# A hybrid decoder step on one core: attention products in three rounded passes, index keys by chunk, sample products at every second tile

## The chip, the cores and the metric

The kernel runs on one core of one Trainium2 chip. Its time is what the device takes for one execution, in microseconds (us). PE is the matrix engine (PEld its loads of the stationary operand), DVE the vector engine, ACT the scalar engine, POOL the general one (GpSimd), SP the engine that issues transfers; SPq, PEq and the like are the sequencers of these engines.

## The reference

One layer of a decoder trunk is applied to a prompt of 2048 tokens and to 8 single-token samples with paged caches. All is float32. What matters here, cut from the reference:

```python
qkv, z, beta_in, a_in, aq, ak, av, iq, ik, iw = split(h @ w_in, cuts)      # h: normed, modulated x
o_gdn = gated delta rule(conv(qkv), ...)                                   # 4 heads of 128
# sparse attention, 4 query heads on 2 key heads of 128, by blocks of 128 queries
score = einsum('bqh,bqhs->bqs', iw, relu(einsum('bqhd,bsd->bqhs', iq, ik)))   # 8 index heads of 64
_, idx = top_k(where(key_pos <= qpos, score, -inf), 256)
p = softmax(q @ k[idx] * 128 ** -0.5);  o_att = p @ v[idx]
x = x + ga1 * (concat(o_gdn, o_att) @ w_out)
x = x + ga2 * ((silu(gate) * up) @ w_ffn_out),  gate, up = split(norm(x) @ w_ffn_in)
```

The kernel does not gather keys: it computes all scores up to the diagonal and adds a bias of -1e30 where a key was not selected.

## The kernel before

**Tiling.** The prompt is worked in four groups of 512 tokens; attention in 16 query blocks of 128. A float32 operand that goes to the large products is split in two parts: `hi`, the value rounded to the format fp32r, and `lo`, the rest. A product is then three passes, hi·hi, hi·lo and lo·hi, in `mm3` (L180, L181, L182). Each weight tile of 128 x 512 is loaded raw (`wr`, two buffers), rounded by ACT (L163) and subtracted by DVE (L164) into `wi` (three buffers). One weight tile feeds four banks of PSUM: 12 matmuls of 512 columns, called a tile below.

**Stages.** Phase 1, up to about 1400 us of the span, projects the four groups, runs the delta rule and attends query blocks 0 to 3 (`first_attn`, which borrows buffers of the delta rule). Phase 2 is three streams that are woven together: the output and feed-forward tiles of groups 0 to 2 (`ffn`, the feed), the index scores and top-k of blocks 4 to 15 (`index`), and their attention (`attend`). The samples' own steps run beside them. Group 3's feed comes last, alone, from about 3130 us, since it needs the attention of block 15. With it the samples' rows go through the same weights.

**Attention (`attend`).** For each of two key heads and each chunk of up to 512 keys, two query heads are multiplied in plain float32 (L1671); the DVE adds the bias and takes the maximum out of PSUM (L1672); ACT takes the exponential. Then, for every two key blocks, PE transposes the four probability tiles into a PSUM bank (L1700), ACT copies the bank to `PT` (L1703), and PE multiplies the values in plain float32, one matmul of 256 columns per key block (L1688). The values of a pair come one pair later (`held`), so that the copy has the time of the next transposes. The values of four key blocks are loaded at a time into `V` (three buffers), a chunk of keys into `kT` (three buffers). The index keys of the whole prompt lie in eight tiles of SBUF that are loaded once, at the start of phase 2.

**Last group.** Each raw weight tile is kept for the samples in a ring of eight buffers (`raw`: `wr`, and `kT` and `V`, which attention no longer needs). `beside` puts four matmuls with 32 stationary columns (L1811) into a list, and `tick`, called after each tile, runs up to two entries of that list.

**What sets the order.** PE's order is written by `weave`: each stream yields its estimated PE time and what it needs of PSUM and of DVE and ACT, and the planner takes the next stream that is ready. The feed may go first while the attention streams have spent more than a share of `PACE` us. PE runs in exactly this order. The other engines take their instructions in the order that a scheduler gives them; each runs its own in order. All transfers are issued by SP, one after the other.

## Time and profile before

| | us |
|---|---|
| median of 3 runs (3690.44 to 3701.23) | 3693.47 |
| the profiled execution's own time | 3695.31 |
| its span, first to last instruction | 3693.2 |
| PE busy in the span | 3430.8 (93%) |
| DVE, ACT, POOL busy | 2083.7, 1476.0, 595.6 |
| mean granted PE clock | 0.967 of full speed |

The profile lists matmul records: a plain float32 matmul leaves two, an fp32r one leaves one. A record's duration is longer than the distance to the next start, since matmuls are pipelined; what one costs a busy PE is read from the starts. In a timeline row `x4` means four records merged.

### The profile page before, as it was taken

To read this page: it belongs to the slowest core of one execution; us is meant where nothing else is said; L and a number is where in the kernel's file an instruction comes from. 1 tells how busy PE (TensorE), PEld (TensorE's weight loads), DVE (VectorE), ACT (ScalarE), POOL (GpSimd) and SP (SyncE) were. 2 spreads that over 40 slices of the span, in tenths; PEclk is the share of its full clock that TensorE was granted. 3 is DMA by queue.
4 is the path that set the end of the run, shared out by engine and by line. 5 is a ranking of instruction groups with operands and counts; after the bars stand their busy time and mean duration, and the time that the engine had idled before them with its cause. 6 is when DMAs were issued, how large, how long until landed. Compare 5 with 4: busy or idle time off the path is not lost.

```text
span 3693.2 us, 62968 instructions
## 1 busy us (share of the span) xinstructions
PE 3430.8 (93%) x23441; PEld 2646.3 (72%) x23441; DVE 2083.7 (56%) x4377; ACT 1476.0 (40%) x2868; POOL 595.6 (16%) x548
## 2 busy tenths in 40 slices
PE   7999999999998898989988999999899999899997
PEld 5867778777766776777766677787677777677775
DVE  3656646636644665666667545666665653443434
ACT  3333323423334323344456534564544633322222
POOL 0001000101001023212210122222022111211213
PEclk8999999999999898999999999999999999999998
DMA  6754565565575225455544453335423233432221
GB/s 240 247 206 164 184 239 190 177 234 180 183 265 189 72 93 162 125 165 155 156 150 141 132 176 104 108 98 175 141 90 98 82 103 106 168 106 81 81 80 62
DMA packets 412270, 545.52 MB, mean 148 GB/s; under 512 B 47364, under 2 KB 285225, under 8 KB 411946
## 3 DMA queue, kind: packets, MB, share of 16 engines
q1 hardware_dynamic: 411954, 541.41, 45.6%
q8 instruction: 186, 3.05, 0.3%
q14 instruction: 130, 1.06, 0.1%
HBM read 435.49 MB, written 124.75 MB: 152 GB/s over the span
## 4 chain that ended last, share of the span: by engine, by line
PE 74%; DVE 9%; DMA 6%; issue 5%; ACT 4%; SPq 1%; POOL 1%; DVEq 0%; ACTq 0%; POOLq 0%
PE d L180 18%; PE d L182 16%; PE d L181 16%; PE s L1626 3%; PE g L1688 3%; PE s L1671 2%; DVE wi L164 1%; PE g L1700 1%; PE g L1811 1%; DVE tm L1768 1%; DMA wi<-kept 1%; ACT bias L1500 1%; PE g L1058 1%; ACT wi L163 1%; PE g L1112 1%
## 5 line engine op out<-in xcount | busy, mean ns | idle before, releaser
L180 PE MATMUL d<-hh,wi 128*128 128x512 f32 x1792 | 780.6, 436 | 32.5 <-DVE tm L1768 15.2
L181 PE MATMUL d<-hl,wi 128*128 128x512 f32 x1792 | 710.2, 396 | 4.7 <-DVE hl L415 3.3
L182 PE MATMUL d<-hh,wi 128*128 128x512 f32 x1792 | 709.8, 396 | 0.0
L164 DVE TENSOR_TENSOR wi<-wr,wi 128x512 fp32r<-128x512 f32 x537 | 394.5, 735 | 485.4 <-ACT wi L163 478.5
L163 ACT CAST wi<-wr 128x512 fp32r<-128x512 f32 x537 | 332.2, 619 | 788.7 <-PE d L182 558.0
L180 PEld LDWEIGHTS d<-hh,wi 128*128 128x128 f32 x1792 | 342.3, 191 | 133.4 <-issue 27.7
L182 PEld LDWEIGHTS d<-hh,wi 128*128 128x128 f32 x1792 | 341.2, 190 | 77.8 <-DVE wi L164 0.8
L181 PEld LDWEIGHTS d<-hl,wi 128*128 128x128 f32 x1792 | 343.1, 191 | 73.3 <-issue 9.1
L1769 POOL TENSOR_TENSOR xt<-xt,tm 128x512 f32<-128x512 f32 x192 | 279.0, 1476 | 433.5 <-DVE tm L1768 384.4
L180 PE MATMUL d<-wi,hh 128*128 128x512 f32 x768 | 325.3, 424 | 24.6 <-DMA wi<-kept 11.0
L180 PE MATMUL d<-wi,ah 128*128 128x512 f32 x704 | 302.6, 430 | 20.0 <-DVE tm L1768 9.0
L181 PE MATMUL d<-wi,hh 128*128 128x512 f32 x768 | 301.8, 393 | 0.4 <-DVE wi L164 0.4
L182 PE MATMUL d<-wi,hl 128*128 128x512 f32 x768 | 302.2, 393 | 0.0
L182 PE MATMUL d<-wi,al 128*128 128x512 f32 x704 | 282.7, 401 | 3.3 <-POOL al L1940 2.6
L181 PE MATMUL d<-wi,ah 128*128 128x512 f32 x704 | 282.1, 401 | 0.0
L1940 POOL TENSOR_TENSOR al<-ca,ah 128x512 fp32r<-128x512 f32 x88 | 119.3, 1369 | 847.1 <-ACT ah L1939 577.5
L1635 DVE SCALAR_TENSOR_TENSOR sc<-rl,iw,sc 128x512 f32<-128x512 f32 (+3 forms) x224 | 167.5, 748 | 80.4 <-ACT rl L1628 74.6
L1628 ACT ACTIVATE rl<-s 128x512 f32<-128x512 f32 (+3 forms) x288 | 150.1, 544 | 147.0 <-PE s L1626 137.0
L180 PEld LDWEIGHTS d<-wi,hh 128*128 128x128 f32 x768 | 145.4, 189 | 74.2 <-DMA wi<-kept 16.5
L1768 DVE TENSOR_TENSOR tm<-d,row 128x512 f32<-128x512 f32 x224 | 152.1, 685 | 69.0 <-PE d L182 49.4
L180 PEld LDWEIGHTS d<-wi,ah 128*128 128x128 f32 x704 | 135.1, 192 | 69.8 <-DVE tm L1768 15.5
L1500 ACT ACTIVATE bias<-sc,sv 128x640 bf16<-128x640 f32 (+11 forms) x120 | 169.7, 1414 | 27.1 <-DVE sv L1502 12.8
(529 smaller groups left out, 5449.8 us busy)
## 6 DMA issues: line engine op xcount, KB each, us to landing
wi<-kept SPq DMA_DIRECT2D x168, 512.0 KB
wr<-in_w_ffn_in_dram SPq DMA_DIRECT2D x572, 128.0 KB
wr<-in_w_ffn_out_dram SPq DMA_DIRECT2D x143, 256.0 KB
kept<-wi SPq DMA_DIRECT2D x56, 512.0 KB
xt<-in_x_prompt_dram SPq DMA_DIRECT2D x8, 2048.0 KB
row<-in_w_ada_dram SPq DMA_DIRECT2D x32, 512.0 KB
wr<-in_w_in_dram SPq DMA_DIRECT2D x56, 256.0 KB
kT<-kT_d SPq DMA_DIRECT2D x54, 256.0 KB
```

What stands on the lines that cost most here:

```text
L163: nc.scalar.copy(w[:, 0], wr)
L164: nc.vector.tensor_tensor(w[:, 1], wr, w[:, 0].bitcast(F32), op=OP.subtract)
L180: self.o(nc.tensor.matmul(out, wh, xh, start=start, stop=False, **kw))
L181: self.o(nc.tensor.matmul(out, wh, xl, start=False, stop=False, **kw))
L182: self.o(nc.tensor.matmul(out, wl, xh, start=False, stop=stop, **kw))
L1500: nc.scalar.activation(c, s, AF.Sign, bias=t, accum_out=cnt)
L1626: self.o(nc.tensor.matmul(ps[:, :w], iq[:, h, :].bitcast(F32R), B["ikT"][c * 2 + a][:, :w].bitcast(F32R), start=a == 0, stop=a == 1))
L1628: nc.scalar.activation(r[:, :w], ps[:, :w], AF.Relu)
L1635: nc.vector.scalar_tensor_tensor(s, r[:, :w], iw, s, op0=OP.mult, op1=OP.add)
L1768: nc.vector.tensor_tensor(tm, pd, rw, op=OP.mult)
L1769: (nc.vector if soon else nc.gpsimd).tensor_tensor(xt, xt, tm, op=OP.add)
L1940: nc.gpsimd.tensor_tensor(al[b], a, ah[b].bitcast(F32), op=OP.subtract)
```

## The change

**Attention in three passes.** In phase 1 the keys and values are split when they are projected: ACT rounds (two copies of 256 columns per token block), POOL subtracts (two), and both parts go to DRAM (`kT_d` and `V_d` double). `attend` splits a block's queries once (ACT into `qh`, POOL in place) and calls `mm3` for the scores and for the values. The probabilities are rounded by ACT's copy out of PSUM, and a new DVE subtraction (L1704) writes their low part into the second half of `PT`.

**Buffers and transfers.** `kT` now holds both parts of a chunk (two buffers for three), `V` both parts of two key blocks for four (three buffers, a transfer for each key block), `PT` is twice as wide. Index keys are loaded by chunk for every query block (`ik`, two buffers, L1618), and the eight resident tiles are gone.

**Last group.** The ring of raw tiles has nine places, two of them second halves of `kT`. `tick` runs up to four entries, at even tiles only. `PACE` goes from 463 to 418, and the planner's costs of the changed steps are new.

```diff
-MM, TP, F4, LAG, EARLY, PACE, GONE_BY = 0.23, 0.46, 0.88, 0.6, 3000, 463, 1e9
+MM, TP, F4, LAG, EARLY, PACE, GONE_BY = 0.23, 0.46, 0.88, 0.6, 3000, 418, 1e9
...
+            v = self.m("vv")[:, :512]
+            for x, hi, lo in ((q[:, :256], q[:, 256:], q[:, :256]), (a[:, 256:512], v[:, :256], v[:, 256:])):
+                nc.scalar.copy(hi.bitcast(F32R), x)
+                nc.gpsimd.tensor_tensor(lo.bitcast(F32R), x, hi, op=OP.subtract)
...
-        return dict(pool=p, kT=one("kT", 512, KR), V=one("V", 512, KR), ikT=self.ikT, qT=one("qT", 512), iqT=one("iqT", 1024), sc=one("sc", T + 18, 2),
+        return dict(pool=p, kT=one("kT", 1024, 2), V=one("V", 512, KR), ik=one("ik", 1024, 2), qT=one("qT", 512), qh=one("qh", 512), iqT=one("iqT", 1024), sc=one("sc", T + 18, 2),
                     bias=one("bias", T, 2, BF), big=one("big", T, 2), rl=one("rl", 512, 2),
-                    PT=one("PT", 512, 2), oT=one("oT", 512, OB))
+                    PT=one("PT", 1024, 2), oT=one("oT", 512, OB))
...
+                ik = B["ik"]().rearrange("p (a n) -> p a n", a=2)
+                nc.sync.dma_start(ik[:, :, :w], self.ikT_d[:, :, c * 512:c * 512 + w].rearrange("a p n -> p a n"))
...
+        qh, ql = B["qh"]().rearrange("p (h n) -> p h n", h=H).bitcast(F32R), qT.bitcast(F32R)
+        nc.scalar.copy(qh, qT)
+        nc.gpsimd.tensor_tensor(ql, qT, qh.bitcast(F32), op=OP.subtract)
...
-                    self.o(nc.tensor.matmul(ps[:, :w], qT[:, h, :], kT[:, :w], start=True, stop=True))
+                    self.mm3(ps[:, :w], qh[:, h, :], ql[:, h, :], kT[:, 0, :w], kT[:, 1, :w], True, True)
...
-                    kb = b0 + b
-                    self.o(nc.tensor.matmul(po[:, :256], V[:, kb % 4, :],
-                                     PT[:, b * 256:(b + 1) * 256], start=kb == 0, stop=kb == i))
+                    kb, s = b0 + b, slice(b * 256, (b + 1) * 256)
+                    self.mm3(po[:, :256], V[:, b, 0], V[:, b, 1], PT[:, 0, s], PT[:, 1, s], kb == 0, kb == i)
...
+                V = B["V"]().rearrange("p (t x c) -> p t x c", t=2, x=2)
+                for b in range(nb):
+                    nc.sync.dma_start(V[:, b], self.V_d[(b0 + b) * 128:(b0 + b + 1) * 128, :, kv * 128:(kv + 1) * 128])
...
+                nc.scalar.copy(PT[:, 0, :nb * 256], pt[:, :nb * 256])
+                nc.vector.tensor_tensor(PT[:, 1, :nb * 256], pt[:, :nb * 256], PT[:, 0, :nb * 256].bitcast(F32), op=OP.subtract)
...
-            while side and (end or n < 2 and at[0] - at[1] >= side[0][0]):
+            while side and (end or n < 4 and at[0] % 2 == 0 and at[0] - at[1] >= side[0][0]):
...
-            tag = ("wr", "kT", "V", "kT", "wr", "V", "kT", "V")[ring[0] % 8]
+            n = ring[0] % 9
+            tag = ("wr", "V", "kT", "", "V", "wr", "V", "kT", "")[n]
```

Three places of the instruction order. The first is PE in phase 2, at the transposes and values of a pair of key blocks (`big` holds the probabilities, `d` are the feed's banks). Before:

```order
L181 MATMUL d<-hl,wi 128x512
L182 MATMUL d<-hh,wi 128x512
L1626 MATMUL s<-ik_15043,iqT 128x512
L1626 MATMUL s<-ik_15045,iqT 128x512
L1700 MATMUL g<-cf,big 128x128 x4
L1688 MATMUL g<-PT,V 128x256 x2
```

With the change:

```order
L1622 MATMUL s<-ik,iqT 128x384 x2
L1700 MATMUL g<-cf,big 128x128 x4
L180 MATMUL g<-PT,V 128x256
L181 MATMUL g<-PT,V 128x256
L182 MATMUL g<-PT,V 128x256
```

The two float32 matmuls of the values have become two sets of three fp32r ones (the second set follows the rows shown). They still stand behind the transposes of the next pair.

The second place is DVE in phase 2, in the last steps of a block's selection (L1515 to L1521 before, L1520 to L1526 after; `tm` belongs to the feed's sums, `wi` to its weights). Before:

```order
L1768 TENSOR_TENSOR tm<-d,row 128x512
L1515 MAX sv<-sc 128x8
L164 TENSOR_TENSOR wi<-wr,wi 128x512
L1518 SCALAR_TENSOR_TENSOR sv<-sv 128x8
L1519 MATCH_REPLACE sc<-sv,sc 128x1936
```

With the change:

```order
L1704 TENSOR_TENSOR PT<-g,PT 128x512
L1769 TENSOR_TENSOR tm<-d,row 128x512
L164 TENSOR_TENSOR wi<-wr,wi 128x512
L1520 MAX sv<-sc 128x8
L1769 TENSOR_TENSOR tm<-d,row 128x512
L1704 TENSOR_TENSOR PT<-g,PT 128x512
L1523 SCALAR_TENSOR_TENSOR sv<-sv 128x8
L1524 MATCH_REPLACE sc<-sv,sc 128x1936
```

The new subtraction L1704 stands between the feed's sums and weight splits and the long passes of the selection.

The third place is PE in the last group (`x` holds the samples, L1811 before is L1818 after). Before, a set of four after every 12 matmuls:

```order
L1811 MATMUL g<-wr,x_32613 32x128 x4
L180 MATMUL d<-hh,wi 128x512
L181 MATMUL d<-hl,wi 128x512
L182 MATMUL d<-hh,wi 128x512
...
L1811 MATMUL g<-V,x_32613 32x128 x4
```

With the change, sets of several tiles after every 24:

```order
L1818 MATMUL g<-kT,x_34042 32x128 x4
L1818 MATMUL g<-V,x_34042 32x128 x4
L1818 MATMUL g<-wr,x_34042 32x128 x4
L180 MATMUL d<-hh,wi 128x512
...
L1818 MATMUL g<-V,x_34042 32x128 x4
L1818 MATMUL g<-kT,x_34042 32x128 x4
```

Over the whole program the 592 sample matmuls stand in 128 unbroken runs before and in 57 with the change.

More of the change, by code (lines that the diff above doesn't have):

```diff
@@ L223, in build @@
             self.iqT_d = self.dr.tile([NB, 128, 8 * 128], F32, name="iqT_d")
-            self.kT_d = self.dr.tile([2, 128, T], F32, name="kT_d")
-            self.V_d = self.dr.tile([T, 256], F32, name="V_d")
+            self.kT_d = self.dr.tile([2, 2, 128, T], F32, name="kT_d")
+            self.V_d = self.dr.tile([T, 2, 256], F32, name="V_d")
             self.ikT_d = self.dr.tile([2, 128, T], F32, name="ikT_d")
@@ L919, in tok @@
             nc.scalar.copy(q[:, :256], pt[:, :256])
-            nc.sync.dma_start(self.kT_d[:, :, tk].rearrange("h p n -> p h n"), q[:, :256].rearrange("p (h n) -> p h n", h=2))
-            nc.sync.dma_start(self.V_d[tk], a[:, 256:512])
+            v = self.m("vv")[:, :512]
+            for x, hi, lo in ((q[:, :256], q[:, 256:], q[:, :256]), (a[:, 256:512], v[:, :256], v[:, 256:])):
+                nc.scalar.copy(hi.bitcast(F32R), x)
+                nc.gpsimd.tensor_tensor(lo.bitcast(F32R), x, hi, op=OP.subtract)
+            for x, part in enumerate((q[:, 256:], q[:, :256])):
+                nc.sync.dma_start(self.kT_d[:, x, :, tk].rearrange("h p n -> p h n"), part.rearrange("p (h n) -> p h n", h=2))
+            nc.sync.dma_start(self.V_d[tk].rearrange("t x c -> t (x c)"), v)
             nc.sync.dma_start(O[2][0, 0, tk].rearrange("n h d -> n (h d)"), a[:, 0:256])
@@ L1527, in phase2 @@
         p = self.p2 = self.pool(es, "p2")
-        self.ikT = []
-        for g in range(self.ng):
-            for a in range(2):
-                k = p.tile([128, GT], F32, name=f"ik{g}{a}")
-                nc.sync.dma_start(k, self.ikT_d[a, :, g * GT:(g + 1) * GT])
-                self.ikT.append(k)
         self.groups(False)
@@ L1595, in first_attn @@
         one = lambda tag, w=512, dt=F32: lambda: p.tile([128, w], dt, name=tag, tag=tag, bufs=2)
-        ikT = []
-        if i0:
-            for a in range(2):
-                ikT.append(p.tile([128, GT], F32, name="gzc", tag="gzc", bufs=2))
-                nc.sync.dma_start(ikT[a], self.ikT_d[a, :, :GT])
-        B = dict(pool=p, kT=one("E"), V=one("AT"), ikT=ikT, qT=one("qe"), iqT=one("qk", 1024), sc=one("ct", 528),
-                 bias=one("dec", 512, BF), big=one("Dm"), rl=one("decb"), PT=one("Y"), oT=one("v"))
+        B = dict(pool=p, kT=one("kq", 1024), V=one("AT"), ik=one("ct", 1536), qT=one("qe"), qh=one("kd"), iqT=one("qk", 1024), sc=one("E", 528),
+                 bias=one("dec", 512, BF), big=one("Dm"), rl=one("decb"), PT=one("qk", 1024), oT=one("v"))
         for i in (i0, i0 + 1):
@@ L1625, in index @@
                     for a in range(2):
-                        self.o(nc.tensor.matmul(ps[:, :w], iq[:, h, :].bitcast(F32R), B["ikT"][c * 2 + a][:, :w].bitcast(F32R), start=a == 0, stop=a == 1))
+                        self.o(nc.tensor.matmul(ps[:, :w], iq[:, h, :].bitcast(F32R), ik[:, a, :w].bitcast(F32R), start=a == 0, stop=a == 1))
                     r = B["rl"]()
@@ L1660, in attend @@
         nc.sync.dma_start(qT, self.qT_d[i].rearrange("p (h n) -> p h n", h=H))
+        qh, ql = B["qh"]().rearrange("p (h n) -> p h n", h=H).bitcast(F32R), qT.bitcast(F32R)
+        nc.scalar.copy(qh, qT)
+        nc.gpsimd.tensor_tensor(ql, qT, qh.bitcast(F32), op=OP.subtract)
+        yield 0, 6, dict(need="s")
         st = p.tile([128, 4, 8], F32, name="st", bufs=2)
@@ L1701, in attend @@
                                             Ps[r][:, (b0 + b) * 128:(b0 + b + 1) * 128], self.id))
-                PT = B["PT"]()
-                nc.scalar.copy(PT[:, :nb * 256], pt[:, :nb * 256])
+                PT = B["PT"]().rearrange("p (x n) -> p x n", x=2).bitcast(F32R)
+                nc.scalar.copy(PT[:, 0, :nb * 256], pt[:, :nb * 256])
+                nc.vector.tensor_tensor(PT[:, 1, :nb * 256], pt[:, :nb * 256], PT[:, 0, :nb * 256].bitcast(F32), op=OP.subtract)
                 if held is not None:
                     values(*held)
-                yield TP * nb / 2 + (F4 if held else 0), 0, dict(act=0.2 + 0.2 * nb, use="g", hold=None if held else "g", need="g")
+                yield TP * nb / 2 + (3 * MM if held else 0), 0, dict(act=0.2 + 0.2 * nb, dve=0.15 + 0.27 * nb, use="g", hold=None if held else "g", need="g")
                 held = b0, nb, V, PT
-            yield 0, 1
+            yield 0, 2
             values(*held)
-            yield F4 * held[1] / 2, 0, dict(need="g")
+            yield 3 * MM * held[1] / 2, 0, dict(need="g")
             pb = self.ps.tile([128, 512], F32, name="g", tag="g", bufs=2)
@@ L1715, in attend @@
             rb = B["PT"]()
+            hi = rb[:, 512:768].bitcast(F32R)
             nc.scalar.copy(rb[:, :256], pb[:, :256])
@@ L1793, in tick @@
                 yield cost, 0
-        side, at, ring = deque(), [0, 0], [0]
+        side, at, ring = deque(), [0, 0], [0, None]
         def raw():
-            tag = ("wr", "kT", "V", "kT", "wr", "V", "kT", "V")[ring[0] % 8]
+            n = ring[0] % 9
+            tag = ("wr", "V", "kT", "", "V", "wr", "V", "kT", "")[n]
             ring[0] += 1
+            if not tag:
+                return ring[1][:, 512:]
+            if tag == "kT":
+                ring[1] = q.tile([128, 1024], F32, name=tag, tag=tag, bufs=2)
+                return ring[1][:, :512]
             pool = wp if tag == "wr" else q
```

13 lines of the change are left out of this document (5 added, 8 removed).

## The prediction, made before the changed kernel was run

> **What bounds the kernel now.** I read the page's busy times and slices first, then the chain of waits.
>
> ```profile
> span 3693.2 us, 62968 instructions
> PE 3430.8 (93%) x23441; PEld 2646.3 (72%) x23441; DVE 2083.7 (56%) x4377; ACT 1476.0 (40%) x2868; POOL 595.6 (16%) x548
> PE   7999999999998898989988999999899999899997
> PE 74%; DVE 9%; DMA 6%; issue 5%; ACT 4%; SPq 1%; POOL 1%; DVEq 0%; ACTq 0%; POOLq 0%
> ```
>
> PE is busy for 93% of the span, in nearly every slice, and is 74% of the chain that ended last; DVE is second with 9%. So PE time that is taken away should shorten the span nearly one for one, unless PE then waits for something else. Next I cut the span at the stages of the program, phase 2 and the last group (columns: the stretch, then busy us of PE, PEld, DVE, ACT, POOL; granted clock, DMA share, GB/s).
>
> ```profile
> 1400.00:3130.00 1730.00, 1615.50 (x7288) 1248.93 (x7287) 1067.62 (x2154) 844.32 (x1476) 335.51 (x291) 0.97 0.42 130
> 3130.00:3693.00 563.00, 526.79 (x3166) 375.33 (x3165) 238.23 (x384) 158.45 (x302) 123.97 (x107) 0.97 0.30 96
> ```
>
> In phase 2 PE lacks 114.5 us of 1730, DVE is 62% busy, and the DMA engines 42%. The waits of that stretch (PE's, then SP's own; total, times, longest) say who holds PE up, and who holds up the transfers:
>
> ```profile
> PE d L180 <- DVE tm L1768: 26.8, 24, 2.9
> PE g L1688 <- ACT PT L1703: 11.1, 6, 3.2
> PE d L180 <- DVE ca L1936: 7.4, 5, 2.3
> ...
> SPq L162 <- DVE wi L164: 559.0, 235, 6.9
> SPq L1696 <- PE g L1688: 130.7, 38, 12.5
> ```
>
> The largest is the feed, which waits for DVE's sums out of PSUM. SP mostly waits because the weights are already loaded as far ahead as their buffers reach.
>
> **The scores.** A stretch of the timeline in which each pair of float32 score matmuls (four records) is followed by one set of three fp32r passes:
>
> ```profile
> 3059.60 1.88 PE L1671 MATMUL s<-kT,qT 128*128 128x512 f32 x4
> 3060.92 0.79 PE L180 MATMUL d<-hh,wi 128*128 128x512 f32 x1
> 3061.55 0.40 PE L181 MATMUL d<-hl,wi 128*128 128x512 f32 x1
> 3061.78 0.40 PE L182 MATMUL d<-hh,wi 128*128 128x512 f32 x1
> 3062.02 1.88 PE L1671 MATMUL s<-kT,qT 128*128 128x512 f32 x4
> ```
>
> One period is 2.42 us. A full fp32r pass starts 0.23 us after the one before (3061.55 to 3061.78), three take 0.69, and so the two float32 matmuls take 1.73, or 0.865 each. In three passes one will take 0.69: 0.175 less. How many there are (two records each):
>
> ```profile
> L1671 PE MATMUL s<-kT,qT x288: 270/592/1219, 1516.5 to 3068.1; 128*128 128x512 f32 x108, 128*128 128x128 f32 x12, 128*128 128x256 f32 x12, 128*128 128x384 f32 x12
> L1671 PE MATMUL s<-E,qe x32: 270/432/697, 703.2 to 1155.2; 128*128 128x128 f32 x8, 128*128 128x256 f32 x8, 128*128 128x384 f32 x8, 128*128 128x512 f32 x8
> L1688 PE MATMUL g<-PT,V x504: 377/379/796, 1540.6 to 3100.9; 128*128 128x256 f32 x168
> L1688 PE MATMUL g<-Y,AT x40: 377/379/796, 711.1 to 1161.2; 128*128 128x256 f32 x40
> ```
>
> For phase 2 the code gives 144 score matmuls: 108 of 512 columns and 12 each of 384, 256 and 128. They save 108 x 0.175 = 18.9 us, and by their columns 12 x (0.131 + 0.087) = 2.6; the narrowest I take at nothing. Together 21.5 us.
>
> **The values.** 252 in phase 2 (504 records). Their float32 pitch, and the pitch of fp32r passes of 256 columns with 128 x 128 stationary, which the index scores already show:
>
> ```profile
> 2903.35 1.03 PE L1688 MATMUL g<-PT,V 128*128 128x256 f32 x4
> 2904.03 0.82 PE L1626 MATMUL s<-ik,iqT 128*128 128x512 f32 x2
> 2904.68 0.39 PE L180 MATMUL d<-wi,ah 128*128 128x512 f32 x1
> ...
> 1549.98 0.64 PE L1626 MATMUL s<-ik,iqT 128*128 128x256 f32 x4
> 1550.45 0.40 PE L180 MATMUL d<-hh,wi 128*128 128x512 f32 x1
> ```
>
> From 2903.35 to 2904.68 is 1.33 us; two full fp32r passes in it are 0.46, so two values matmuls take 0.87, or 0.435 each. Four fp32r passes of 256 columns take 0.47: 0.1175 each, 0.352 for three. That is 0.0825 less, x 252 = 20.8 us. Phase 1 has four scores of each width and 20 values: 4 x (0.175 + 0.131 + 0.087) + 20 x 0.0825 = 3.2 us. The attention products save 45.5 us of PE time.
>
> A rule speaks against this. The Trainium skill (TensorE: Matmul & The Clock Gate, "The mechanism" of its Part 3) says that the load of a stationary operand overlaps running matmuls only where the row groups differ, and its section on LDWEIGHTS gives 128 columns / 1.2 GHz, 107 ns. Then the 432 more loads of the change would cost, by an estimate from that page, 46 us and take the whole saving of the attention products. The pitch of 0.1175 us, with a load for each pass, does not agree; I keep the row.
>
> **The sample products.** In the last group, first a place where the samples of two tiles happen to run together, then one with a single tile's four (eight records):
>
> ```profile
> 3302.76 0.40 PE L182 MATMUL d<-wi,al 128*128 128x512 f32 x1
> 3303.08 0.42 PE L1811 MATMUL g<-wr,x 128*32 128x128 f32 x8
> 3303.33 0.40 PE L1811 MATMUL g<-V,x 128*32 128x128 f32 x8
> 3303.66 0.50 PE L180 MATMUL d<-wi,ah 128*128 128x512 f32 x1
> 3303.99 0.39 PE L181 MATMUL d<-wi,ah 128*128 128x512 f32 x1
> ...
> 3306.32 0.39 PE L182 MATMUL d<-wi,al 128*128 128x512 f32 x1
> 3306.64 0.43 PE L1811 MATMUL g<-kT,x 128*32 128x128 f32 x8
> 3307.00 0.50 PE L180 MATMUL d<-wi,ah 128*128 128x512 f32 x1
> 3307.33 0.40 PE L181 MATMUL d<-wi,ah 128*128 128x512 f32 x1
> ```
>
> From L182 to the next L181 would be 0.46 us without samples. It is 1.01 with one set and 1.23 with two. So a set costs 0.22 us, and each interruption 0.33 us more: the gap ahead of the set and the slower first passes behind it. The order of instructions has 128 runs before and 57 after: 71 x 0.33 = 23.4 us less. The sets themselves stay. At the very end four tiles' samples stand behind the last feed matmul instead of three, with the transpose they need just ahead: about 1 us more, my estimate from the 0.22 us a set and one more wait.
>
> **What is added.** The subtraction L1704: 132 in phase 2, mostly 512 columns out of PSUM. The nearest rows, and the one for POOL:
>
> ```profile
> L1768 DVE TENSOR_TENSOR tm<-d,row 128x512 f32<-128x512 f32 x224 | 152.1, 685 | 69.0 <-PE d L182 49.4
> L1703 ACT COPY PT<-g 128x512 f32<-128x512 f32 (+1 forms) x132 | 74.1, 562 | 47.1 <-PE g L1700 46.9 <-issue 0.2
> L1940 POOL TENSOR_TENSOR al<-ca,ah 128x512 fp32r<-128x512 f32 x88 | 119.3, 1369 | 847.1 <-ACT ah L1939 577.5
> ```
>
> 132 x 0.685 is 90 us of DVE time, which would take DVE from 62% to 1158 of about 1687 us, 69%. None of it is PE time, but L1704 waits for ACT's copy, and the feed's weight splits and sums are queued behind it, while the values now wait for ACT and DVE in series, 0.56 + 0.69 us. The pair of transposes that stands ahead of the values covers that when DVE is free. When DVE is in a long selection pass, `tm` comes later and the feed waits. Bounds: at best the 11.1 us of the values' waits for `PT` go away with the new spacing and nothing comes (-11); at worst the three rows of PE's waits above (45 us) double (+45). DVE's load per unit of idle time rises from 0.62/0.38 to 0.69/0.31, by over a third, which would be +16; with some of the copy waits gone I take +10.
>
> Splitting the queries costs ACT some 0.6 and POOL 1.4 us for each of 12 blocks, and in phase 1 a token block costs two small ones each. Both engines idle for over half of the span; nothing is queued behind them but the block's own first score, and a planner's step lies between. I cost it at nothing; uncovered it is 12 x 2 = 24 us, which I leave to the upper bound.
>
> Transfers: for 126 query-key blocks in phase 2 the keys and the values each add 2 x 64 KB and the index keys 128 KB, 49 MB less the 2 MB no longer loaded at once. That is 27 GB/s on top of 130, so a DMA share of about 0.51 for 0.42. SP issues 180 more value transfers and 28 more for index keys. It spends 559 us of the stretch waiting for the weights' buffers, so it has the time, and I cost this at nothing too. In the last group the ring grows from eight to nine and at most four are held, so five tiles of 2.8 us each are still loaded ahead.
>
> **The sum.** -45.5 - 23.4 + 10 + 1 = -58 us. The profiled execution took 3695.31, 2.1 more than its span and 1.8 over the median of the runs. Against the median that gives 3693.5 - 58 = 3636. I forecast **3637 us**.
>
> **The rivals.**
> DVE becomes the brake: +45 instead of +10, 3672 us. For it: `tm` is already PE's largest wait, and the new work comes in the same stretches as the selection. Against it: DVE keeps 30% idle time, and PE's order is written with the subtraction's cost known.
> The grouped samples save nothing, because the raw tiles they hold delay the weights behind them: 3637 + 23 = 3660 us. For it: the ring is longer by only one place. Against it: no row shows PE waiting for a weight in the last group, and five tiles are some 14 us ahead.
> The loads of the stationary operand show: the change has 432 more matmul records (one for each of 160 scores and 272 values), each with a load. PEld's 2646.3 us over 23441 loads are 0.113 us each; if these lay bare, 49 us, 3686 us, no change. Against it stands the pitch of 0.1175, which leaves no room for a bare load. The rule of the Trainium skill named above would make it so.
> The other side: SP's queue. A value load now covers two key blocks, so the three `V` buffers reach 6 blocks ahead instead of 12, and a load that waits for PE's values holds every weight load behind it. The row shows 38 such waits of 3.4 us on average, 12.5 at the longest. The weights loaded ahead (three `wi`, two `wr`, one in use) cover four tiles of 12 x 0.23, 11 us; above that PE stops. If 60 more value loads waited like the longest, each would cost 1.5 us, 90 us in all: 3727, slower. It decides from 58 us on. Against it: the mean wait is a third of the cover.
>
> **How the numbers follow.** A measurement of this kernel tells about 0.3%, 11 us, from no change. My forecast (3612 to 3658): 0.70. DVE as brake: 0.12. Grouping without gain: 0.08. Loads laid bare: 0.03. SP's queue: 0.04. Something of about no effect in sum that I do not name: 0.03. The first three are faster than 3682, 0.90; same 0.05 (the loads, part of the rest); slower 0.05. The range goes from 3612 (the waits at -11, and 4 us for a slightly better pitch) to 3672 (DVE's bound).
>
> **What would show it.** In the changed profile: the scores as three rows of `mm3` with starts 0.23 us apart, six values passes in 0.70 us; PE busy near 3370 us; in the last group 57 runs of samples, with 0.33 us lost at each, and that stage about 22 us shorter; DVE near 1158 us in phase 2, with L1704 at about 0.69 us, and PE's waits for `tm` around 35 us. I am wrong if PE's idle time in phase 2 rises well over 125 us, if `values` wait for L1704 by tens of us, if SP's waits for the values' buffers reach PE as waits for `wi`, or if an fp32r pass of 256 columns takes much over 0.12 us.

## The result

The changed kernel takes 3715.03 us (median of 5 runs, 3705.72 to 3721.22) against 3693.47 in runs beside it: a ratio of 1.0063, 95% interval 1.0047 to 1.0079. It is slower by 0.6%, where 3637 us were forecast. From the page of the changed kernel, busy times and chain:

```profile
span 3711.9 us, 64512 instructions
PE 3405.7 (92%) x23873; PEld 2688.9 (72%) x23873; DVE 2168.0 (58%) x4521; ACT 1502.7 (40%) x2916; POOL 639.8 (17%) x596
PE 67%; DVE 13%; DMA 8%; issue 5%; ACT 4%; SPq 2%; POOL 1%; DVEq 0%; ACTq 0%; POOLq 0%
```

PE is busy for 25 us less, not for 61, and the span is 19 us longer: PE waits more, and its mean granted clock is 0.958 for 0.967. DVE's share of the chain has grown from 9% to 13%, that of transfers from 6% to 8%. The span cut where the feed of each group starts (phase 1, three groups, last group), first before, then changed; columns as in the prediction. Phase 1 ends here where the first group's feed starts, at 1165 us before, ahead of the 1400 us named above:

```profile
0.00:1165.00 1165.00, 1072.89 (x10305) 845.01 (x10306) 633.95 (x1585) 398.44 (x950) 91.69 (x112) 0.96 0.63 209
1165.00:1880.00 715.00, 638.43 (x4565) 510.36 (x4564) 446.46 (x933) 285.39 (x552) 156.54 (x123) 0.94 0.46 138
1880.00:2524.30 644.30, 616.20 (x2888) 465.43 (x2887) 398.31 (x795) 336.62 (x584) 117.11 (x125) 0.99 0.42 130
2524.30:3155.80 631.50, 599.74 (x2626) 468.15 (x2625) 378.49 (x700) 306.75 (x503) 114.39 (x87) 0.98 0.35 113
3155.80:3693.00 537.20, 503.60 (x3066) 357.31 (x3064) 226.46 (x367) 148.83 (x283) 115.85 (x101) 0.97 0.28 90
```

```profile
0.00:1179.00 1179.00, 1078.05 (x10341) 849.04 (x10342) 650.24 (x1597) 410.79 (x986) 121.53 (x148) 0.96 0.64 213
1179.00:1913.90 734.90, 646.80 (x4650) 519.96 (x4649) 467.59 (x985) 296.48 (x568) 163.79 (x130) 0.92 0.49 149
1913.90:2552.80 638.90, 605.91 (x3019) 473.19 (x3018) 421.25 (x824) 337.41 (x582) 120.41 (x130) 0.98 0.50 155
2552.80:3171.60 618.80, 585.12 (x2807) 478.01 (x2805) 407.49 (x752) 308.70 (x500) 118.12 (x90) 0.98 0.48 149
3171.60:3711.00 539.40, 489.83 (x3063) 368.70 (x3063) 221.42 (x366) 149.32 (x284) 115.96 (x101) 0.96 0.28 89
```

The later two groups are shorter, by 5.4 and 12.7 us. Phase 1 is 14 us longer, the first group 19.9, and the last group has gained nothing. What the parts were forecast to save (scores of 512 columns by group 20, 36 and 52, values 52, 84 and 116, at the prediction's prices) stands beside what came. All stage times below are taken like this: from the start of a group's first feed matmul to the next group's, in phase 1 from the first matmul of all, in the last group to the last feed matmul. Each is of one profile: four kernels with the code of the kernel before up to the last group take 1151.6 to 1158.2 us in phase 1 and lie within 4 us of each other in each of the three groups, and three with the code of the changed one up to there scatter by 3.4 us in phase 1 and 6.2 in the first group.

| us | phase 1 | first | second | third | last |
|---|---|---|---|---|---|
| before | 1158.2 | 715.0 | 644.3 | 631.5 | 515.8 |
| changed | 1172.3 | 734.9 | 638.9 | 618.8 | 519.7 |
| difference | +14.1 | +19.9 | -5.4 | -12.7 | +3.9 |
| forecast, without DVE's +10 | -3.2 | -8.7 | -14.1 | -19.5 | -22.4 |
| forecast missed by | 17.3 | 28.6 | 8.7 | 6.8 | 26.3 |

The last row sums to 87.7; less the 10 forecast for DVE these are the 78 us missed.

**Where it goes in phase 1 and in the first group.** At the ends of both the feed stands, because the next group needs the last attention blocks. These stretches without a feed matmul, called holes below, before and changed:

```profile
1129.40:1165.00 35.60, 28.17 (x128) 18.40 (x127) 11.23 (x39) 17.17 (x41) 2.92 (x5) 0.81 0.65 210
1850.30:1880.00 29.70, 18.82 (x67) 12.52 (x66) 20.13 (x56) 18.21 (x39) 3.35 (x4) 0.71 0.66 234
```

```profile
1123.80:1179.00 55.20, 35.00 (x176) 25.70 (x175) 19.79 (x66) 22.36 (x54) 3.11 (x6) 0.78 0.55 181
1849.40:1913.90 64.50, 45.80 (x179) 32.23 (x178) 47.52 (x118) 39.16 (x76) 7.98 (x9) 0.75 0.63 212
```

They have grown from 36 to 55 us and from 30 to 64. PE's order alone says part of it. Counted at 0.23 us for a matmul of 512 columns, the PE work that is not feed and that stands between the last feed matmul of one group and the first of the next was 7.8 us at the end of phase 1 and is 16.0, and was 4.7 at the end of the first group and is 23.1. The counts before take a plain float32 matmul for one pass; at the prices of the prediction they are about 14 and 8.5. The three-pass operations in the order of the old costs (a run below) leave 12.2 and 7.4. At the end of the first group it was, before, half the scores and the values of one key head of block 7; now it is the end of block 6, both key heads of block 7, and all index scores of block 8, which are 8.3 of the 23.1 us. Alone, such work takes far longer. From the timeline of the 64 us (`g<-cf,big` are the transposes, `g<-PT,V` the values):

```profile
1879.38 1.93 PE L1700 MATMUL g<-cf,big 128*128 128x128 f32 x8
1882.74 0.58 PE L180 MATMUL g<-PT,V 128*128 128x256 f32 x1 [1.43 <-DVE PT L1704]
1883.12 0.41 PE L181 MATMUL g<-PT,V 128*128 128x256 f32 x1
1883.33 0.41 PE L182 MATMUL g<-PT,V 128*128 128x256 f32 x1
1883.54 0.41 PE L180 MATMUL g<-PT,V 128*128 128x256 f32 x1
...
1897.10 0.34 PE L1700 MATMUL g<-cf,big 128*128 128x128 f32 x1 [2.19 <-ACT big L1680]
1898.24 1.35 PE L1700 MATMUL g<-cf,big 128*128 128x128 f32 x7 [0.80 <-ACT big L1680]
1901.19 0.58 PE L180 MATMUL g<-PT,V 128*128 128x256 f32 x1 [1.60 <-DVE PT L1704]
```

PE waits for ACT's copy and DVE's subtraction in series (4.8 us in sum for L1704 in this hole, and 5.6 for ACT's `rl` at the index scores), and then its passes start 0.21 us apart (1883.12, 1883.33, 1883.54). Beside the feed they start 0.12 apart:

```profile
3080.30 0.60 PE L1700 MATMUL g<-cf,big 128*128 128x128 f32 x4
3080.66 0.37 PE L180 MATMUL g<-PT,V 128*128 128x256 f32 x1
3080.86 0.28 PE L181 MATMUL g<-PT,V 128*128 128x256 f32 x1
3080.98 0.28 PE L182 MATMUL g<-PT,V 128*128 128x256 f32 x1
```

So in the hole the clock falls too: 0.75 is granted there, and 0.71 was in the shorter hole before. This fits PE's busy time in the first group, which rose from 638.4 to 646.8 us with less work in it.

**The prices were right.** Between two feed matmuls a pair of 512-column scores costs 1.38 us (median of 21 places of the run with the attention alone) where it cost 1.72 (33 places): 0.17 each. Four transposes with two values cost 1.16 (60 places) for 1.31 (49).

### The profile page after: what moved, and what is told of

Same layout as the page of the kernel before. It is cut to its first block, busy times and chain, and to the rows that moved or that the text cites. A ratio compares the mean times of both kernels' runs of the same rounds, so it can differ in the third digit from the quotient of the medians.

```text
span 3711.9 us, 64512 instructions
## 1 busy us (share of the span) xinstructions
PE 3405.7 (92%) x23873; PEld 2688.9 (72%) x23873; DVE 2168.0 (58%) x4521; ACT 1502.7 (40%) x2916; POOL 639.8 (17%) x596
## 4 chain that ended last, share of the span: by engine, by line
PE 67%; DVE 13%; DMA 8%; issue 5%; ACT 4%; SPq 2%; POOL 1%; DVEq 0%; ACTq 0%; POOLq 0%
PE d L180 17%; PE d L182 15%; PE d L181 15%; PE s L1622 3%; DVE wi L164 2%; DVE tm L1769 2%; DMA wi<-kept 1%; PE g L1700 1%; PE g L1818 1%; DVE ca L854 1%; DMA x_d<-xt 1%; PE g L1063 1%; ACT bias L1505 1%; DMA wr<-in_w_ffn_out_dram 1%; DMA wr<-in_w_ffn_in_dram 1%
## 5 line engine op out<-in xcount | busy, mean ns | idle before, releaser
L180 PE MATMUL d<-hh,wi 128*128 128x512 f32 x1792 | 746.0, 416 | 28.8 <-DVE tm L1769 16.9
L182 PE MATMUL d<-hh,wi 128*128 128x512 f32 x1792 | 708.5, 395 | 0.0
```

The costliest lines, as they stand in the source:

```text
L180: self.o(nc.tensor.matmul(out, wh, xh, start=start, stop=False, **kw))
L182: self.o(nc.tensor.matmul(out, wl, xh, start=False, stop=stop, **kw))
```

## Experiments: the grouping of the samples

**Grouping alone.** The kernel before with only this:

```diff
-            while side and (end or n < 2 and at[0] - at[1] >= side[0][0]):
+            while side and (end or n < 4 and at[0] % 2 == 0 and at[0] - at[1] >= side[0][0]):
```

> The kernel before with the grouping of the samples alone (up to four sets behind every second tile), its ring of eight raw tiles unchanged. Theory A (grouping saves 0.33 us at each of about 71 interruptions, but the raw tiles it holds make the next weights late, and gives all of it back): 3688 to 3698 us, with ACT's casts in the last group waiting for the weights' transfers for over 20 us in sum. Theory B (grouping brings what the prediction says, and the loss of the whole change lies in the attention alone): 3670 us, casts waiting under 8 us. Theory C (grouping does harm by itself): above 3700 us.

Measured: 1.0031 (1.0021 to 1.0041), 3701.83 us, slower, the last group 525.4 us for 515.8. Its waits in the last group, for the weights' transfers:

```profile
ACT wi L163 <- DMA wr<-in_w_ffn_in_dram: 43.7, 6, 8.3
ACT wi L163 <- DMA kT<-in_w_ffn_in_dram: 23.4, 4, 14.0
ACT wi L163 <- DMA wr<-in_w_ffn_out_dram: 6.4, 1, 6.4
```

In the kernel before the same waits are 4.9 us in all. The time falls just into theory C's range; the waits are theory A's mechanism, though all of the gain and more is gone.

**A longer ring.** The same with fourteen raw tiles:

```diff
-            tag = ("wr", "kT", "V", "kT", "wr", "V", "kT", "V")[ring[0] % 8]
+            tag = ("wr", "kT", "V", "PT", "rl", "kT", "V", "wr", "qT", "kT", "V", "PT", "rl", "oT")[ring[0] % 14]
```

> As the run with the grouping alone, but with a ring of fourteen raw tiles: the buffers of the attention (PT, rl, qT, oT), which nothing uses in the last group, are put in between. Theory A (late weights took the gain): 3668 to 3676 us, the waits of the casts for transfers back under 8 us, the last group about 20 us shorter than before. Theory B: the same 3670 us as without the longer ring. Theory C (the interruption is not what costs, so that grouping has no gain to give): within 5 us of the run with eight tiles.

Measured: 0.9992 (0.9980 to 1.0005), the last group 512.7 us. The waits for late weights fell from 73.5 us to 22.1, and still the stage is only 3 us shorter than before, so the time lies between the theories. Over the stage, and above 0.23 us a step, the runs of sample matmuls and the slower steps behind them cost 49.8 us for 71.9 before, 22 less; but steps over 0.4 us between two feed matmuls cost 22.9 us for 6.3, so that nearly 17 come back. PE's waits for `tm` are 14.6 us for 0.5. They stand where DVE's sums have to empty the four banks before the next tile can use them. DVE's timeline at one such place (`tm<-g` is the samples' own sum, `tm<-d` are the sums that empty the feed's four banks):

```profile
3306.06 0.29 DVE L1768 TENSOR_TENSOR tm<-g,sc 128x128 f32<-128x128 f32 x1 [1.92 <-PE g L1811]
3306.27 0.68 DVE L1768 TENSOR_TENSOR tm<-d,row 128x512 f32<-128x512 f32 x1
3306.86 0.68 DVE L164 TENSOR_TENSOR wi<-wr,wi 128x512 fp32r<-128x512 f32 x1
3307.46 0.68 DVE L1768 TENSOR_TENSOR tm<-d,row 128x512 f32<-128x512 f32 x1
```

DVE stands 1.92 us for the samples' matmuls, which PE now runs in a bundle behind the last feed matmul. The four banks' sums stand behind it in DVE's queue, and the next tile waits for its banks.

**The sum one step later.**

```diff
-                after(0, 0, out)
+                after(1, 0, out)
```

> The kernel before with the grouping and the ring of fourteen, and the samples' own sum (tm<-g) put one step later: it no longer runs in the same tile as the sets it sums, so DVE doesn't stand waiting for them in front of the four sums that empty the feed's banks. Theory D (the interruptions do cost less, and the waits at the ends of the passes behind that sum, 13.5 us in the last group, take it back): 3674 to 3679 us, the steps over 0.4 us between feed matmuls in the last group gone. Theory E (a set of samples costs what it costs however they are grouped, and the waits merely show it elsewhere): 3685 to 3690 us, as with the ring of fourteen alone.

Measured: 0.9964 (0.9952 to 0.9976), 3678.3 us, the last group 503.0 us. In time theory D holds. Its sign does only in part: the steps over 0.4 us cost 17.9 us, still 11.6 more than before, so that 13 of the 25 us saved at the samples are left. Bundles of one to four sets cost 0.45, 0.66, 0.88 and 1.10 us, and 0.11 more at the next step: 0.22 a set and 0.33 an interruption, as forecast.

**The whole change with the old rule, and with a longer ring.**

```diff
-            while side and (end or n < 4 and at[0] % 2 == 0 and at[0] - at[1] >= side[0][0]):
+            while side and (end or n < 2 and at[0] - at[1] >= side[0][0]):
```

> The changed kernel with the old rule for the samples (up to two sets behind each tile) and its ring of nine: the attention part of the change alone. Theory A (grouping is worth nothing with nine tiles): 3710 to 3720 us, as the whole change. Theory B (grouping brings 23 us and the attention loses all the more): 3738 us. Theory C (grouping does harm): 3700 to 3705 us. All three have the boundaries between the groups as late as in the changed kernel: about 37 us lost by the start of the second group's feed, against the kernel before.

```diff
-            tag = ("wr", "V", "kT", "", "V", "wr", "V", "kT", "")[n]
+            tag = ("wr", "V", "kT", "", "PT", "rl", "ik", "qT", "V", "wr", "V", "kT", "", "PT", "rl", "ik", "qh", "oT")[n]
```

> The changed kernel with eighteen raw tiles in the last group in place of nine (the attention's dead buffers put in between), all else as it is. Theory A (late weights took the grouping's gain): 3690 to 3697 us, about 20 less than the changed kernel, all of it in the last group, with the waits of ACT's casts for transfers there under 10 us (51 us in the changed kernel) and PE's waits for tm there under 3 us (15.9). Theory B (the buffers are not what holds the last group up, but DVE's order is): 3710 to 3717 us.

Measured: 1.0056 (1.0039 to 1.0073) for the attention alone: the change's loss is the attention's, and its grouping is worth nothing. With eighteen tiles 1.0040 (1.0027 to 1.0054): 8 us of the change's 23 come back, not 20, between the theories. The samples' sum still stands in front there, and PE's waits for `tm` are 14.6 us for 16.6.

## Experiments: the attention

**Old costs.** All new operations, with the planner told the old prices (likewise 1 us ahead of the last values, no 6 us ahead of a block, `PACE` at 463), and the old rule for the samples:

```diff
-                    yield 0.1 + 0.6 * w / 512, 0, dict(dve=0.2 + 0.6 * w / 512, use="s", need="s")
+                    yield F4 * w / 512, 0, dict(dve=0.2 + 0.6 * w / 512, use="s", need="s")
...
-                yield TP * nb / 2 + (3 * MM if held else 0), 0, dict(act=0.2 + 0.2 * nb, dve=0.15 + 0.27 * nb, use="g", hold=None if held else "g", need="g")
+                yield TP * nb / 2 + (F4 if held else 0), 0, dict(act=0.2 + 0.2 * nb, use="g", hold=None if held else "g", need="g")
```

> The changed kernel's attention, operation for operation, with the old rule for the samples, but with the planner told the costs of the kernel before (0.88 us a score and a pair of values, no DVE time for the subtraction, no 6 us ahead of a block, 1 us ahead of the last values, 463 in all): the order of PE's work then leaves 7.5 us of other work at the end of the first group's feed (4.7 before, 23 with the new costs). Theory A (the order written by the new costs puts the attention too late against the feed, and its saving is lost uncovered at the ends of the groups): 3665 to 3685 us, the loss at the start of the second group's feed under 10 us. Theory B (the new operations themselves, the subtraction on DVE and the split of the queries on ACT, are too slow for any order): 3700 us or more, with as long a hole at that place.

Measured: 1.0073 (1.0051 to 1.0095), 3717.73 us. The stages are 1161.1, 722.4, 652.0, 636.0 and 515.5 us: phase 1 is mended and the first group's hole is back at 35 us, but the later groups lost what they had gained. Theory A falls as it stood; theory B has the time, but not the hole. PE's largest waits in the first group:

```profile
PE g L180 <- DVE PT L1703: 22.0, 4, 7.0
PE d L180 <- DVE tm L1768: 16.0, 13, 2.6
```

The values (`g`) wait for the subtraction, up to 7 us at a time.

**No subtraction.** The changed kernel, and then the one with the old costs, each with

```diff
-                nc.vector.tensor_tensor(PT[:, 1, :nb * 256], pt[:, :nb * 256], PT[:, 0, :nb * 256].bitcast(F32), op=OP.subtract)
...
-                    self.mm3(po[:, :256], V[:, b, 0], V[:, b, 1], PT[:, 0, s], PT[:, 1, s], kb == 0, kb == i)
+                    self.mm3(po[:, :256], V[:, b, 0], V[:, b, 1], PT[:, 0, s], PT[:, 0, s], kb == 0, kb == i)
```

> The changed kernel without the subtraction L1704: the low part of the probabilities is left out and the second pass multiplies the high part again, so PE does the same work in the same order and DVE 132 subtractions less in phase 2. Theory A (the order at the ends of the groups is the cause): 3705 to 3712 us, the same holes a few us shorter. Theory B (DVE's new 90 us are the brake): 3680 us or less.

> The order of the kernel before (old costs, old rule for the samples) and no subtraction: the low part of the probabilities is left out and the high part multiplied twice, so PE does the same work. Theory F (two things took the attention's saving, DVE's subtraction and an order that runs late, each enough by itself to take most of it): 3648 to 3665 us, PE's waits for PT under 15 us in phase 2 (43 with the subtraction). Theory G (the fp32r passes are not as short in a row as the single rows say, and nothing was saved): 3690 us or more.

Measured: 0.9965 (0.9949 to 0.9982), 3680.1 us, for the first: the subtraction costs the changed kernel 36 us (0.98% of 3690), most of it in the first and third groups (718.7 and 602.4 us). Theory B has this time to 0.1 us; phase 1 stays late, 1176.8 us. For the second 1.0036 (1.0024 to 1.0049), 3705.87 us: theory F falls there, and so does theory G, which has the time, but not the price of the passes (0.17 us less a score). With the old costs the subtraction costs some 14 us. With the old order nothing is gained even without the subtraction; its values then wait for ACT's copy at the same places:

```profile
PE g L180 <- ACT PT L1702: 17.1, 5, 6.2
```

As I read it, the attention stands as early in that order as before, and the PE work around it has shrunk, so PE arrives before the exponentials and copies are done.

**The query split later.** The change with the old sample rule and

```diff
+        yield 0, 6
         nc.scalar.copy(qh, qT)
         nc.gpsimd.tensor_tensor(ql, qT, qh.bitcast(F32), op=OP.subtract)
-        yield 0, 6, dict(need="s")
+        yield 0, 3, dict(need="s")
```

> The changed kernel with the old rule for the samples, and the copy that splits the queries issued 6 us behind their load in place of right after it, so that ACT does not stand in its queue for the transfer (20 us in 10 waits in the changed kernel). Theory A (the order at the ends of the groups): 3703 to 3712 us, little below the 3710 of the attention alone. Theory C (ACT's standing for the queries holds the feed and the selection up, and makes the attention late): 3690 us or less.

Measured: 1.0106 (1.0075 to 1.0138), 3730.26 us: 19 us slower than the same without this. The first group takes 738.9 us (728.7 without) and the second 651.6 (637.3). But the edit does not do what it was meant to. ACT's waits for the queries of blocks 4 to 15, first with the old sample rule alone, then with the later split:

```profile
ACT qh L1658 <- DMA qT<-qT_d: 16.4, 7, 6.0
ACT qh L1659 <- DMA qT<-qT_d: 20.3, 7, 6.4
```

With phase 1's they are 20.9 us and 28.3: ACT stands longer, not shorter. So theory C is not tested by this run, and what costs the 19 us is not shown.

**Scores only.** Old costs, old sample rule, the values as before the change (`PT` and `V` in float32, no L1704):

```diff
-                    self.mm3(po[:, :256], V[:, b, 0], V[:, b, 1], PT[:, 0, s], PT[:, 1, s], kb == 0, kb == i)
+                    self.o(nc.tensor.matmul(po[:, :256], V[:, kb % 4, :],
+                                     PT[:, b * 256:(b + 1) * 256], start=kb == 0, stop=kb == i))
```

> Scores in three rounded passes, values in float32 as in the kernel before (so no subtraction of probabilities on DVE and no split V), old costs, old rule for the samples, the key tiles three deep. Theory F (what costs no DVE time is gained): 3670 to 3678 us, 21.5 us of PE time less and little else changed. Theory G (no gain from the passes): 3690 us or more; theory C (the split of the queries on ACT costs what the passes bring): 3685 to 3692 us.

> The scores alone in three passes, with the samples grouped, the raw ring lengthened to twenty and the samples' own sum one step later. If the gains add: 14 us below the run with the scores alone, 3655 to 3665 us. If the grouping's gain needs something the kernel before had in the last group: equal to the run with the scores alone.

> Scores alone in three passes, values in float32, grouping mended as above, and the order of phase 2 written with the new cost of a score and the 6 us ahead of a block. If the saving of the scores arrives when the order knows of it: 3660 to 3670 us. If the order is not the point and the first group's selections are the bound: 3676 to 3684 us, as the same kernel with the old costs (3681).

Measured: 1.0004 (0.9994 to 1.0015), 3690.55 us: none of the 21.5 us. Theory F falls; G and C both have this time, and the price of the passes speaks against G. C stays open: the split of the queries is in this kernel, and so are the index keys loaded by chunk, and no run takes either out alone. With the mended grouping 0.9970 (0.9956 to 0.9985), and with the new cost of a score 0.9975 (0.9959 to 0.9991): both are what the grouping alone gives (0.9964), so the scores add nothing to it, whichever costs the order was written with. The first of them lies between its two forecasts (3681.28 us); the second has the time of "the order is not the point" (3679.13), but that selections are the bound there is put in doubt by the last run below. With the new costs the first group is 707.1 us and the second 663.0: the gain of the one is the loss of the other.

**A quarter of the weights' subtractions on POOL**, with old costs and the old sample rule:

```diff
-        nc.vector.tensor_tensor(w[:, 1], wr, w[:, 0].bitcast(F32), op=OP.subtract)
+        (nc.gpsimd if self.turn % 4 == 3 else nc.vector).tensor_tensor(w[:, 1], wr, w[:, 0].bitcast(F32), op=OP.subtract)
```

> The full attention of the change with the old costs and the old rule for the samples, and in phase 2 every fourth weight's low part subtracted on POOL in place of DVE: some 110 to 148 subtractions of 0.69 us off DVE, about what L1704 puts on it. Theory F (DVE's capacity is what the values wait for): 3665 to 3690 us, PE's waits for PT under 20 us. Theory H (the delay is in the chain from transpose to copy to subtraction to values, not in DVE's load): 3710 us or more.

Measured: 1.0041 (1.0026 to 1.0056), 12 us less than with the old costs alone (the intervals just overlap), between the theories.

## Experiments: the parts put right together

**Mended.** The changed kernel with the old costs in blocks 0 to 3 (and without the 6 us ahead of a block there), the ring of eighteen and the samples' sum later:

```diff
-                    yield 0.1 + 0.6 * w / 512, 0, dict(dve=0.2 + 0.6 * w / 512, use="s", need="s")
+                    yield (F4 * w / 512 if i < 4 else 0.1 + 0.6 * w / 512), 0, dict(dve=0.2 + 0.6 * w / 512, use="s", need="s")
```

> The changed kernel with three things mended: in blocks 0 to 3 (phase 1) the planner is told the old costs, the raw ring of the last group has eighteen tiles, and the samples' own sum runs one step later. If the parts add as the runs so far show them (about 15 us at the end of phase 1, 8 for the ring, 13 for the sum), 3676 to 3684 us. If the loss at the end of phase 1 only moves into the first group (whose selections would then be the bound), 3690 us or more.

> As the mended kernel, without the subtraction L1704 (the low part of the probabilities is left out, the high part multiplied twice). Theory I (DVE's subtraction costs about 35 us in any order that is written for three passes, and with it, the phase 1 order and the grouping's faults the account closes): 3640 to 3650 us, near the forecast. Theory J (without the late phase 1 the first group has no slack to lose, and the subtraction hides): within 12 us of the mended kernel.

> As the mended kernel, with every fourth weight's low part in phase 2 subtracted on POOL in place of DVE (some 148 subtractions of 0.69 us off DVE). If DVE's load is what costs, most of the 35 us come back: 3650 to 3662 us. If it is the longer chain from transposes to values, or if POOL holds DVE up when both work: 3672 us or more.

> As the run with every fourth weight's subtraction on POOL, with every second. If DVE's load is still what costs: 3655 to 3666 us. If a quarter was enough: within 4 us of that run. If POOL's subtractions, 1.4 us for DVE's 0.69, make the weights late or hold DVE up: 3680 us or more.

Stage times of these runs, and the hole at the end of the first group (29.7 us before, 64.5 changed):

| us | ratio (95% interval) | phase 1 | first | second | third | last | hole |
|---|---|---|---|---|---|---|---|
| mended | 0.9967 (0.9954 to 0.9981) | 1156.8 | 718.5 | 641.1 | 622.9 | 502.7 | 63.8 |
| and no subtraction | 0.9928 (0.9903 to 0.9952) | 1163.2 | 719.2 | 636.0 | 620.3 | 502.1 | 59.6 |
| and a quarter on POOL | 0.9939 (0.9919 to 0.9958) | 1163.3 | 719.9 | 638.8 | 612.4 | 504.6 | 63.4 |
| and half on POOL | 1.0010 (0.9997 to 1.0022) | 1168.4 | 731.6 | 637.6 | 624.1 | 501.3 | 68.5 |

(Phase 1 has the same code in the first, third and fourth rows: the 11.6 us between them are what single profiles scatter by.) The parts add: the mended kernel takes 3679.35 us, and with a quarter of the weights' low parts on POOL 3670.69, between the theories. That one beats the kernel before by 0.6%, but the mended grouping alone by 0.25% only, and their intervals meet. Taken out of this order the subtraction is worth 0.39%, 14 us (11 by the medians), not 36: theory J is nearer than I. Half on POOL loses that gain and 17 us more; POOL needs 1.32 us for each where DVE needs 0.76, from the groups of the run with half:

```profile
L166 DVE TENSOR_TENSOR wi<-wr,wi 128x512 fp32r<-128x512 f32 x218 | 166.1, 762 | 233.9 <-ACT wi L164 232.5
L166 POOL TENSOR_TENSOR wi<-wr,wi 128x512 fp32r<-128x512 f32 x217 | 286.9, 1322 | 893.2 <-ACT wi L164 757.2 <-issue 37.3 <-DVE sc L1633 35.4
```

DVE's own subtractions take 762 ns each (744 in the run with a quarter), and PE's waits for `tm` in phase 2 rise from 18.2 to 27.1 us. Which queue makes them late was not tried.

**The first group.** Its hole of 64 us remains in all four. The last run asks whether the selections' chain sets the group's length:

```diff
-        for k in range(SEARCH):
+        for k in range(6 if 512 < n <= 1024 else SEARCH):
```

> The mended kernel with six steps of the search for the threshold in blocks 4 to 7 in place of ten (four steps are left out there, so the selected keys are found less exactly; PE's work is the same). If the chain of the selections bounds the first group (about 2 us a step, four blocks of which two stand in series): the first group 16 to 25 us shorter than the mended kernel's 718.5 us, the hole ahead of the second group's feed 64 to under 45 us, 3655 to 3665 us. If PE or the transfers bound it: within 6 us of the mended kernel.

With six steps some rows are not selected exactly, the kernel's general path then runs the index scores, the attention and the feed a second time, and the whole takes 7727.42 us; the first pass through the groups can still be read. The hole shrinks to 37.2 us, and yet the group takes longer, 726.8 for 718.5 (first this run, then the mended kernel):

```profile
1170.50:1897.30 726.80, 639.74 (x4650) 519.55 (x4649) 456.40 (x935) 276.93 (x533) 159.94 (x129) 0.93 0.50 150
1163.70:1882.20 718.50, 642.04 (x4650) 516.37 (x4649) 467.26 (x982) 296.25 (x568) 161.02 (x128) 0.93 0.50 152
```

PE is busy as long as in the mended kernel (642.0 us) and waits inside the group instead. Neither theory has this time, and the planner's order changes with the shorter search. So the chain of the selections does not set this group's length by itself, and the hole is not the measure of the loss. What keeps the group at 711 to 739 us in nearly every order stays open; only the scores alone with the new costs went below (707.1), and lost it again in the second group.

## Why the prediction was wrong

**"PE time that is taken away should shorten the span nearly one for one".** This is the step that failed first. The prices of the products were right (0.17 us saved a score for 0.175, 0.075 a value for 0.0825), and the later two groups did give 18 of 34 us. At the ends of phase 1 and of the first group PE time is not the bound: the order was rewritten with the new costs, put the attention later against the feed, and left 16 and 23 us of PE work uncovered where the order of the old costs leaves 12 and 7 of the same operations. Uncovered, this work waits for ACT and DVE and runs at a lower clock. I looked at the order in three places, where the products stand, and not at the ends of the groups, where it could be counted before anything ran; and the stretch from 1400 us on that I examined leaves out the end of phase 1.

In phase 1 this is shown: with the old costs in blocks 0 to 3 the hole is 35 us again, and phase 1 takes 1156.8 to 1168.4 us in four profiles, for 1172.3 to 1175.7 with the new order and 1151.6 to 1158.2 with the code before. In the first group it is not: the mended kernel leaves as long a hole there, 63.8 us, and its first group is still 16 us shorter than the changed one's. PE idles in it as long as before the change (718.5 less 642.0 us, before 715.0 less 638.4); what is missing is that its busy time did not fall by the forecast 8.7 us. And with phase 1 and the grouping mended and without the subtraction the ratio is 0.9928, with the mended grouping alone 0.9964, so the attention then gives some 13 of its 45 us. Where the other 32 went, the first group's share among them, stays open.

**Grouping, -23.4.** The 0.33 us an interruption held, but the step "five tiles are still loaded ahead" did not: held tiles come free in bursts, and ACT waited 54 us for transfers in the changed kernel's last group. That raw tiles held for the samples delay the weights was a rival, given 0.08. Unforeseen was the second half, the samples' sum that stands before the banks' sums in DVE's queue. In the change the grouping gave nothing; with both mended it gives 13 us.

**DVE, +10.** That the subtraction costs PE time by its place in DVE's queue and in the values' chain was right, the size was not: 36 us in the changed kernel, inside the bound of +45 that I gave a chance of 0.12. DVE's load came out nearly as forecast (1142 us in the stretch, forecast 1158), and so did its time of 0.68 us:

```profile
L1704 DVE TENSOR_TENSOR PT<-g,PT x132: 405/684/694, 1577.3 to 3147.1; 128x512 fp32r<-128x512 f32 x120, 128x256 fp32r<-128x256 f32 x12
```

What failed was to price it by load and by the waits for `tm`. These fell, 26.8 to 15.2 us; the new waits are spread over others in the same stretch:

```profile
PE d L180 <- DVE tm L1769: 15.2, 15, 2.5
PE d L180 <- DVE th L1941: 11.2, 7, 3.5
PE g L1700 <- DVE PT L1704: 10.9, 9, 2.8
PE d L180 <- ACT ah L1946: 9.4, 2, 8.2
ACT qh L1658 <- DMA qT<-qT_d: 16.2, 6, 6.3
```

These rows do not add up to 36 us, and which wait carries the price is not shown. It hangs on the order: 36 us in the changed kernel's, 14 in the mended one and with the old costs.

**The split of the queries, nothing.** ACT does stand in its queue for the load (last row). In PE's longest wait for `ah`, 8.2 us, ACT stood 4.0 us for the queries, with `ah` queued behind them. "Nothing is queued behind them but the block's own first score" was wrong. What this costs in all is open, since the run with the later split did not take the standing away.

**Transfers and stationary loads, nothing.** Nearly right. The DMA share in the stretch is 0.51, as forecast, and in the whole run PE waits 2.0 us for values, 1.7 for keys and 2.2 for index keys. Passes of 256 columns with a load each start 0.12 us apart beside the feed. The rule of the Trainium skill that I weighed (TensorE: Matmul & The Clock Gate, "The mechanism" of Part 3), that a load overlaps running matmuls only where the row groups differ, would have laid these loads bare; this pitch does not agree with it. The same section also lets a load into the background weight buffer go ahead, which I passed over.

## What to carry to other kernels

When an order is written from costs, changing a price moves every stage: count, from the order itself, how much work is left uncovered at the ends of the stages before taking a saving in the middle at its face value. What an operation between two engines in a chain costs can differ from order to order (36 and 14 us here for the same subtraction), and its engine's load does not tell it, so measure it in the order that will be used. When an experiment is to take a wait away, make sure from its trace that the wait is gone before reading its time. Work that is bundled holds its buffers longer and makes its consumer wait at one place: lengthen the ring, and keep what waits for the bundle out of the queue that frees the next pass.

## What the runs showed of the hardware

PE's pace halved without a long wait: the passes from 1882.74 us on start 0.21 us apart where 0.12 is the pitch beside the feed, and in the 14 us before them no wait is longer than 1.43 us. It had halved in the same hole at 1863 us already (score passes 0.43 apart), after waits of at most 2.07 us. The granted clock is 0.75 over the 64.5 us, in which PE is busy for 45.8. The Trainium skill (TensorE: Matmul & The Clock Gate, "HAM oscillation — how this bites in real kernels") gives as its abstract rule no idle gaps over some 3.4 us; no wait here is that long. Between the two the pace was full (scores 0.23 apart), from the same timeline:

```profile
1873.34 0.39 PE L181 MATMUL s<-kT,qh 128*128 128x512 f32 x1
1873.57 0.40 PE L182 MATMUL s<-kT,qT 128*128 128x512 f32 x1
1873.80 0.63 PE L1622 MATMUL s<-ik,iqT 128*128 128x512 f32 x2
1875.12 1.68 PE L1622 MATMUL s<-ik,iqT 128*128 128x128 f32 x8 [0.69 <-ACT rl L1624]
1877.66 1.92 PE L1622 MATMUL s<-ik,iqT 128*128 128x128 f32 x8 [0.86 <-ACT rl L1624]
```
